# Strassen's seven block products for the Gelu half of two up-projections, with weight sums made by adding transfers

## The chip, the cores and the metric

One core of a Trainium2 chip runs the whole program. The metric is the device time in microseconds of one execution; several executions are made, and their median is given. The profile is of one execution, and its times are microseconds from the first instruction (ns where marked). TensorE (PE; PEld is its weight load) multiplies into PSUM banks, ScalarE (ACT) and VectorE (DVE) do the element work, GpSimd (POOL) and SyncE (SP) mostly issue transfers here.

## The reference, cut to what matters

A decoder trunk of two layers for 512 tokens of 1024 features: layer 0 mixes tokens by dilated attention, layer 1 by a gated recurrence, and each is followed by this block, wrapped in RMS norms and added to the residual stream:

```
def conv_ffn(x, w_up, conv_w, conv_b, w_down):
    u = causal_dwconv(x @ w_up, conv_w, conv_b)
    g, v = u[..., :D_FF], u[..., D_FF:]
    return (jax.nn.gelu(g, approximate=True) * v) @ w_down
```

`D_FF` is 3072, so `w_up` is 1024 x 6144. Its first 3072 columns feed the Gelu half, the others the value half. The convolution runs along the tokens and has three taps per feature.

## The kernel before

**Products in three passes.** An fp32 operand is split into a high part (`hi`, a ScalarE copy to fp32r) and the remainder (`lo`, a VectorE subtraction); `split` (L148) does both. A product is then hi x hi + hi x lo + lo x hi, three matmuls (`mm3`, L257). The activations `hT` are kept transposed, features on the partitions in 8 blocks of 128, the 512 tokens along the free side, and are split once per projection. The weights are split as they arrive.

**The weight stream.** `plan` lists all weight chunks in order. A chunk of the up-projection is 1024 x 256 (1 MB, one transfer by `load`, L193, on SP's queue, into one of three `raw` buffers). `pump` (L167) cuts a loaded chunk into two units of 1024 x 128, splits them (two instructions of 512 elements on ScalarE and two on VectorE per unit) and keeps up to eight units (`W_UNITS`). `take` hands out a unit, `done` gives its place back, and `tick` (L222), called after every output tile, steps the side jobs in `sides` and then calls `pump`. The schedule is manual: every engine works through its instructions in the order in which the program writes them, and waits are on what the program wrote before.

**The up-projection.** `ffn` (L591) runs over 12 pairs j: a Gelu chunk of 256 columns and the value chunk that belongs to it. `feat_tiles` (L433) makes four output tiles of 128 features x 512 tokens, each 8 x 3 matmuls into a PSUM bank of its own, of eight. In the first pair the tokens are halved, 256 columns a matmul. After each tile comes `sink` (L607): `conv` (L594) reads the bank with one ScalarE instruction and two VectorE ones; a Gelu tile then gets its activation on ScalarE (L611), a value tile is multiplied into the Gelu tile on VectorE (L615). The results `gv` (24 tiles) are split again for the down-projection, `rows_run` (L475), which takes 12 chunks of rows and ends in the norms that read and write the residual `x_sb`.

Small tiles of 512 columns come from a pool of 32 (`gen`); `gain` tiles hold norm weights; GpSimd's queue carries gains and the token transposes through memory.

Of the kernel before, what the change touches and what calls it, by code (L numbers as in the profile page):

```python
# [18 lines left out]
P = 128  # L19
S = 512  # L20
D = 1024
# [53 lines left out]
def kernel(  # L75
# [38 lines left out]
    def nm(s):  # L114
        uid[0] += 1
        return f"{s}{uid[0]}"
# [11 lines left out]

    ident = cp.tile([P, P], F32, tag="ident", name="ident")
    make_identity(nc, ident)  # L130
    x_sb = cp.tile([P, 4, D], F32, tag="x_sb", name="x_sb")

    def gain(src, layer, eng=nc.gpsimd):
        g = cp.tile([P, D], F32, tag="gain", name=nm("gain"), bufs=2)
# [19 lines left out]
    raws, units, pieces = {}, {}, []  # L154
    sides, first_w, first_y, one = [], [], [], []

    def parts_of(kind, raw):

        if kind == "feat":
            return [raw[:, :, m * P : (m + 1) * P] for m in range(2)]  # L160
        if kind == "value":
            return [raw[:, 2 * i : 2 * i + 2, :] for i in range(2)]
        if kind == "rows":
            return [raw[:, i : i + 1, :] for i in range(2)]
        return [raw]

    def pump(limit=2):  # L167

        for _ in range(limit):
            i = state["cv"]  # L170
            if not pieces and i < state["dma"]:
                pieces.extend((i, j, u) for j, u in enumerate(parts_of(plan[i][0], raws.pop(i))))
                state["cv"] += 1
            if pieces and state["live"] < W_UNITS:
                i, j, raw = pieces.pop(0)
                hi, lo = (
                    wp.tile([P] + list(raw.shape[1:]), F32R, tag=t, name=nm("w" + t)) for t in ("hi", "lo")
                )
                h = raw.shape[1] // 2
                cuts = [(slice(None), slice(0, h)), (slice(None), slice(h, 2 * h))]  # L180
                if raw.shape[1] == 1:
                    cuts = [(slice(None), slice(0, 1), slice(n, n + 512)) for n in (0, 512)]
                if plan[i][4] is not None:
                    split_normed(hi, lo, raw, plan[i][4] + (2 * j if plan[i][0] == "value" else 0))
                    cuts = []
                for c in cuts:
                    split(hi[c], lo[c], raw[c])
                units[i, j] = (hi, lo)
                state["live"] += 1
            while not pieces and state["dma"] < len(plan) and state["dma"] - state["cv"] < RAW_BUFS:  # L190
                load()

    def load():  # L193
        i = state["dma"]
        kind, kd, cols, srcs = plan[i][:4]
        raw = wp.tile([P, kd, cols], F32, tag="raw", name=nm("raw"), bufs=RAW_BUFS)
        at = 0
        for src, n in srcs:
            nc.sync.dma_start(raw[:, :, at : at + n] if kind == "value" else raw[:, at : at + n, :], src)
            at += n  # L200
        raws[i] = raw
        state["dma"] += 1

    def chunk():
        i = state["next"]
# [10 lines left out]
    def done(n=1):  # L216
        state["live"] -= n
# [16 lines left out]
        while sides:  # L234
            tick()

    def w_cols(w, c0, normed=False):
# [4 lines left out]
        plan.append(("feat", KD, 256, srcs, 0 if normed else None))  # L242

    def w_value(w, *cuts):

# [37 lines left out]
    def halves(ap):  # L283
        return [ap[:, 0:512], ap[:, 512:1024]]
# [28 lines left out]
        return t.rearrange("p (b n i) -> p n b i", b=4, i=32)  # L313

    def prenorm(t, hT, g, wait):
        xh, gh = halves(x_sb[:, t, :]), halves(g)
# [31 lines left out]
    def first_transposed(t, i):  # L348

        ps = psum("tr")  # L350
        for k in range(4 * i, 4 * i + 4):
            nc.tensor.transpose(
                ps[:, k % 4 * P : (k % 4 + 1) * P],
                x_sb[:, t, i * 512 : i * 512 + 512].rearrange("t (p k) -> t k p", k=4)[:, k % 4], ident,
            )
        first_split(t, i, ps)

# [14 lines left out]
    def first_squares(i):  # L372
        for t in range(4):
            junk = gen(s="junk")
            nc.scalar.activation(
                junk, x_sb[:, t, i * 512 : i * 512 + 512], AF.Square, accum_out=first_ss[i][:, t : t + 1]
            )

    def first_roots():
# [20 lines left out]
    def postnorm(t, banks, g, final):  # L400
        at = [slice(0, 512), slice(512, 1024)]
        parts = banks
        u = [gen(s="post") for _ in at]

        def gained(i):
            nc.vector.tensor_tensor(u[i], parts[i], g[:, at[i]], op=ALU.mult)

        y = rms(parts, gained)
        for i, c in enumerate(at):
            xc = x_sb[:, t, c]  # L410
# [180 lines left out]
    def ffn(layer, hT, post, pre):  # L591
# [25 lines left out]
        order = [([0, 1, 2, 3], range(9)), ([0], range(9, 12)), ([1], range(9, 12))]  # L617
        order += [([2, 3], [9]), ([2], [10, 11]), ([3], [10, 11])]
        prep, run = rows_proj(12, act_split(gv), order, post, pre)
        for j in range(12):  # L620
            if j == 11:
                prep(3)
            feat_tiles(2, hT, lambda b, ps: sink(b, ps, j), j == 0)
        return run()


    def attention(hT, post, pre):
# [436 lines left out]
    for layer in range(2):  # L1064
# [7 lines left out]
            for c in range(4):  # L1072
                w_rows(lru_w_out[0], c * 256)
        for j in range(12):
            w_cols(ffn_w_up[layer], j * 256)
# [12 lines left out]

    def x_half(t, i):
        c = slice(i * 512, (i + 1) * 512)  # L1090
        nc.sync.dma_start(x_sb[:, t, c], x[0, t * P : (t + 1) * P, c])

    def w_part(i, k0, k1):
        nc.sync.dma_start(raws[i][:, k0:k1, :], plan[i][3][0][0][:, k0:k1, :])
# [69 lines left out]
```

## Time and profile before

| | |
|---|---|
| median of 3 runs | 1455.94 us (1455.89 to 1456.03) |
| profiled execution | span 1454.0 us from first to last instruction; 1.9 us of the median lies around it |
| TensorE busy | 1445.0 us, 99% |
| VectorE / ScalarE / GpSimd busy | 61% / 46% / 9% |
| mean granted TensorE clock | 0.999 |
| read from / written to memory | 156.24 MB / 15.29 MB |

How to read the rows that follow: a group's row gives line, engine, operation, output<-inputs, shapes and count, then busy time and mean ns of one, then the idle time of its engine just before, with what ended it. A chain row gives start, length, and what. A window row gives, for a stretch, its length and each engine's busy time with its count, then the granted clock, the transfer engines' share and GB/s. A timeline row gives start, length, engine, line, operation and count, in brackets the idle time before and its releaser. A tile's row gives the shortest, median and longest duration in ns. A busy PE includes matmuls that overlap; what a matmul costs is read from the distance between starts.

### The profile page before, as it was taken

The numbers are of one execution on the slowest core, as the hardware profiler recorded it, in microseconds if no ns is written. First come the engines' busy times: TensorE is split into PE (matmuls) and PEld (weight loads), VectorE is DVE, ScalarE is ACT, GpSimd is POOL, SyncE is SP. The second block draws the span as 40 slices with busy tenths as digits, with TensorE's granted clock in tenths as the row PEclk, the third lists the DMA queues.
The fourth block names the chain that finished last, engine by engine and source line by source line (L and its number), as shares of the span: only waits on it lengthen the run. The fifth ranks groups of instructions, "written<-read, shape, count | busy, mean of one in ns | idle before, by whom it ended". The sixth has DMA issues, their size and how long they took to land.

```text
span 1454.0 us, 18793 instructions
## 1 busy us (share of the span) xinstructions
PE 1445.0 (99%) x6861; PEld 1214.4 (84%) x6861; DVE 879.8 (61%) x1955; ACT 675.9 (46%) x1532; POOL 133.9 (9%) x275
## 2 busy tenths in 40 slices
PE   9999999999999999999999999999999999999998
PEld 7888888888888898888888888888898888888886
DVE  6767747474735975555564338769775555564333
ACT  7656636262615553343444335589453434444221
POOL 0340414040402100000000001000100000000000
PEclk9999999999999999999999999999999999999999
DMA  7653637372726343323323322432333233223201
GB/s 225 207 146 109 174 113 208 104 215 97 216 96 211 102 131 100 103 87 102 101 88 116 115 73 88 131 116 84 120 102 116 87 102 102 87 104 128 88 0 58
DMA packets 125364, 172.76 MB, mean 119 GB/s; under 512 B 8736, under 2 KB 102392, under 8 KB 125272
## 3 DMA queue, kind: packets, MB, share of 16 engines
q1 hardware_dynamic: 114280, 145.48, 31.0%
q0 software_dynamic: 10144, 25.04, 5.9%
q8 instruction: 54, 0.88, 0.2%
q10 hardware_dynamic: 848, 1.05, 0.2%
q14 instruction: 38, 0.31, 0.1%
HBM read 156.24 MB, written 15.29 MB: 118 GB/s over the span
## 4 chain that ended last, share of the span: by engine, by line
PE 93%; ACT 4%; DVE 3%; issue 1%; DVEq 0%; ACTq 0%
PE ps L259 55%; PE acc L259 24%; PE v L758 8%; PE v L688 1%; DVE xb L967 1%; PE O L909 1%; PE S L854 1%; PE S L808 1%; DVE wlo L150 1%; ACT sig L988 1%; ACT whi L149 1%; PE O L259 1%; PE tr L341 1%; ACT sig L1007 0%; ACT a L1005 0%
## 5 line engine op out<-in xcount | busy, mean ns | idle before, releaser
L259 PE MATMUL ps<-hT,whi 128*128 128x512 f32 (+1 forms) x2752 | 801.3, 375 | 0.0
L259 PEld LDWEIGHTS ps<-hT,whi 128*128 128x128 f32 x2752 | 503.6, 188 | 91.6
L259 PE MATMUL ps<-hT,wlo 128*128 128x512 f32 (+1 forms) x1376 | 515.3, 374 | 0.0
L150 DVE TENSOR_TENSOR wlo<-raw,whi 128x512 fp32r<-128x512 f32 x360 | 230.8, 686 | 187.2 <-ACT whi L149 187.1
L259 PEld LDWEIGHTS ps<-hT,wlo 128*128 128x128 f32 x1376 | 259.1, 188 | 46.5
L149 ACT ACTIVATE whi<-raw 128x512 fp32r<-128x512 f32 x360 | 204.6, 621 | 135.4 <-PE acc L259 121.0
L600 DVE SCALAR_TENSOR_TENSOR u<-ps,cols,u 128x511 f32<-128x511 f32 x192 | 143.8, 749 | 140.6 <-ACT u L596 137.2
L259 PE MATMUL acc<-whi,ahi 128*128 128x512 f32 x512 | 199.7, 390 | 0.0
L259 PE MATMUL acc<-whi,alo 128*128 128x512 f32 x512 | 199.4, 389 | 0.1
L259 PE MATMUL acc<-wlo,ahi 128*128 128x512 f32 x512 | 199.3, 389 | 0.0
L143 ACT ACTIVATE whi<-raw,first_w 128x128 fp32r<-128x128 f32 (+1 forms) x432 | 146.2, 425 | 56.6 <-PE ps L259 33.9
L596 ACT ACTIVATE u<-ps,cols 128x512 f32<-128x512 f32 x96 | 74.8, 779 | 210.0 <-PE ps L259 210.0
L144 DVE SCALAR_TENSOR_TENSOR wlo<-raw,first_w,whi 128x128 fp32r<-128x128 f32 (+1 forms) x432 | 139.5, 389 | 1.4 <-ACT whi L143 1.3
L259 PEld LDWEIGHTS acc<-whi,alo 128*128 128x128 f32 x512 | 96.1, 188 | 20.5 <-DVE alo L150 0.5
L259 PEld LDWEIGHTS acc<-whi,ahi 128*128 128x128 f32 x512 | 96.1, 188 | 19.8
L259 PEld LDWEIGHTS acc<-wlo,ahi 128*128 128x128 f32 x512 | 96.2, 188 | 19.8
L758 PE MATMUL v<-whi,hT 128*128 128x512 f32 x320 | 102.4, 393 | 0.0
L302 POOL DMA_DIRECT2D turned<-T x36 | 19.6, 547 | 763.4 <-DVE T L296 759.9
L309 POOL DMA_DIRECT2D ft<-turned x144 | 78.7, 554 | 39.6 <-issue 17.7
L758 PEld LDWEIGHTS v<-whi,hT 128*128 128x128 f32 x320 | 60.1, 188 | 12.3
L611 ACT ACTIVATE u<-u 128x512 f32<-128x512 f32 x48 | 30.3, 632 | 80.4 <-DVE u L600 80.4
L758 PE MATMUL v<-wlo,hT 128*128 128x512 f32 x160 | 62.3, 389 | 0.0
(171 smaller groups left out, 1010.7 us busy)
## 6 DMA issues: line engine op xcount, KB each, us to landing
raw<-in_ffn_w_up_dram SPq DMA_DIRECT2D x48, 1024.0 KB
raw<-in_attn_w_qkv_dram SPq DMA_DIRECT2D x67, 512.0 KB
raw<-in_ffn_w_down_dram SPq DMA_DIRECT2D x24, 1024.0 KB
raw<-in_lru_w_in_dram SPq DMA_DIRECT2D x8, 1024.0 KB
turned<-T POOLq DMA_DIRECT2D x28, 256.0 KB, 2.6
ft<-turned POOLq DMA_DIRECT2D x112, 64.0 KB, 5.8
vrows<-v SPq DMA_DIRECT2D x16, 256.0 KB
vp<-vrows SPq DMA_DIRECT2D x16, 256.0 KB
```

Of the source, the lines that this page charges most:

```text
L143: nc.scalar.activation(hi[:, k], raw[:, k], AF.Copy, scale=w)
L144: nc.vector.scalar_tensor_tensor(lo[:, k], raw[:, k], w, hi[:, k].bitcast(F32), op0=ALU.mult, op1=ALU.subtract)
L149: nc.scalar.activation(hi, raw, AF.Copy)
L150: nc.vector.tensor_tensor(lo, raw, hi.bitcast(F32), op=ALU.subtract)
L259: mm(dst, l[a], r[b], start=start and n == 0, stop=stop and n == 2)
L302: nc.gpsimd.dma_start(d, T)
L309: nc.gpsimd.dma_start(t[32 * c : 32 * c + 32].rearrange("j (b x) -> j b x", b=4), d.rearrange("(b j) (c x) -> c j b x", j=32, c=4)[c],)
L341: nc.tensor.transpose(ps[:, k * P : (k + 1) * P], xs[i][:, k * P : (k + 1) * P], ident)
L596: nc.scalar.activation(u, ps, AF.Identity, scale=cc[:, j : j + 1], bias=cc[:, 48 + j : 49 + j])
L600: nc.vector.scalar_tensor_tensor(u[:, d:], ps[:, : S - d], wc, u[:, d:], op0=ALU.mult, op1=ALU.add)
L611: nc.scalar.activation(u, u, AF.Gelu_apprx_tanh)
L758: mm(banks[t], hT[a][:, k, t * P : (t + 1) * P], W[b][:, k % 2, :], start=(k, a, b) == (0, 0, 0), stop=(k, a, b) == (KD - 1, 1, 0),)
```

## The change

In pairs 3 to 10 of both up-projections the Gelu product (1024 x 256 weights by 1024 x 512 activations) is made from 2 x 2 blocks by seven block products, not eight, in Winograd's form. A block of the weights is 512 x 128, a block of the activations 512 x 256 tokens. Four sums of activation blocks (`T`) are made once per layer by a side job, `token_sums`, in place of the residual, which goes out to memory meanwhile and comes back before pair 11 (`x_back`). Four sums of weight blocks are made per pair: `c += d` by an adding transfer from memory when the chunk is loaded, `a += c` and `b += a` by adding transfers within SBUF, and `a - d` by VectorE. The Gelu chunk then has four units, made in the order first value unit, `first`, `second`, `third`, `fourth`, second value unit. The products share two PSUM banks, `y[0]` and `y[1]`: the left 256 columns accumulate, are copied, negated and go on accumulating (`p5`, `z`, `c()` from `-a()`), and the right 256 columns are written by VectorE. Between the products stand the value chunk's quarters a to h (six matmuls of 512 columns each).

```diff
+SEVEN = range(3, 11)
...
+    def summed(i, raw):
+
+        a, b, c, d = (raw[:, 4 * k : 4 * k + 4, m * P : m * P + P] for m, k in ((0, 0), (0, 1), (1, 0), (1, 1)))
+        shape = [KD, P]
+
+        def first(hi, lo):
+            two = [h.rearrange("p (k m) c -> p k (m c)", m=2) for h in (hi, lo)]
+            split(*two, raw[:, 0:4, :])
+            add_rows(a, c)
+
+        def second(hi, lo):
+            split(hi, lo, raw[:, :, 0:P])
+            add_rows(b, a)
+            nc.vector.tensor_tensor(a, a, d, op=ALU.subtract)
+
+        def third(hi, lo):
+            split(hi, lo, raw[:, :, 0:P])
+
+        def fourth(hi, lo):
+            split(hi[:, 0:4], lo[:, 0:4], d)
...
         for _ in range(limit):
             i = state["cv"]
-            if not pieces and i < state["dma"]:
-                pieces.extend((i, j, u) for j, u in enumerate(parts_of(plan[i][0], raws.pop(i))))
-                state["cv"] += 1
+            if not pieces and i + (i < len(plan) and plan[i][0] == "wino") < state["dma"]:
+                if plan[i][0] == "wino":
+                    u, v = summed(i, raws.pop(i)), [
+                        plain(i + 1, j, r) for j, r in enumerate(parts_of("feat", raws.pop(i + 1)))
+                    ]
+                    pieces.extend([v[0], *u, v[1]])
+                    state["cv"] += 2
...
+        if kind == "wino":
+            add_rows(raw[:, 0:4, P:256], srcs[0][0][:, 4:8, P:256])
         raws[i] = raw
         state["dma"] += 1
+
+    def add_rows(to, src):
+        nc.gpsimd.dma_start(to, src, accum_op=ALU.add)
...
         for j in range(12):
+            if j == 1:
+                side(token_sums(hT, T))
             if j == 11:
+                x_back()
                 prep(3)
-            feat_tiles(2, hT, lambda b, ps: sink(b, ps, j), j == 0)
+            if j in SEVEN:
+                seven(hT, T, lambda b, ps: sink(b, ps, j))
+            else:
+                feat_tiles(2, hT, lambda b, ps: sink(b, ps, j), j == 0)
         return run()
 
+    kept = []
+
+    def x_back():
+
+        X[0] = cp.tile([P, 4, D], F32, tag="x_sb", name=nm("x_sb"))
+        nc.gpsimd.dma_start(X[0], kept.pop())
+
+    def token_sums(hT, T):
+
+        assert len(sides) == 1
+        d = dp.tile([P, 4, D], F32, name=nm("x_kept"))
+        nc.gpsimd.dma_start(d, X[0])
+        kept.append(d)
+        homes = cp.tile([P, 4, D], F32R, tag="x_sb", name=nm("T"))
+        homes = [homes[:, n] for n in range(4)]
+        homes += [cp.tile([P, D], F32R, tag="gain", name=nm("T"), bufs=2) for _ in range(2)]
+        homes = [[h[:, 0:512], h[:, 512:1024]] for h in homes]
+        homes += [[gen(F32R, "T") for _ in range(2)] for _ in range(2)]
+        homes = [[h.rearrange("p (k t) -> p k t", k=2) for h in hs] for hs in homes]
+        yield 1
+
+        def both(k0, n):
+            o = gen(s="B").rearrange("p (k t) -> p k t", k=2)
+            hi, lo = (h[:, k0 : k0 + 2, n * 256 : n * 256 + 256] for h in hT)
+            nc.gpsimd.tensor_tensor(o, hi.bitcast(F32), lo.bitcast(F32), op=ALU.add)
+            return o
+
+        tt = nc.vector.tensor_tensor
+        B = {}
+        for k in range(2):
+            for n, at in (((0, 0), 2 * k), ((0, 1), 2 * k), ((1, 1), 4 + 2 * k), ((1, 0), 4 + 2 * k)):
+                B[k, n] = both(at, n[1])
+        yield 2
+        for k in range(2):
+            b11, b12, b22, b21 = (B[k, n] for n in ((0, 0), (0, 1), (1, 1), (1, 0)))
+            tt(b11, b11, b12, op=ALU.subtract)
+            tt(b12, b12, b22, op=ALU.subtract)
+            tt(b22, b22, b11, op=ALU.add)
+            tt(b21, b21, b22, op=ALU.subtract)
+            yield 1
+            for n, b in enumerate((b11, b22, b12, b21)):
+                split(homes[2 * n][k], homes[2 * n + 1][k], b)
+            if not k:
+                yield 1
+        T.extend([homes[2 * n], homes[2 * n + 1]] for n in range(4))
+
+    def seven(hT, T, sink):
+
+        i, iv = chunk(), chunk()
+        t = gen(s="part")
+        y, v = {}, {}
...
+        left = {
+            1: (0, pairs(0), block(0, 0), 0), 5: (0, pairs(1), turn(0), 1), 6: (1, row(0), turn(1), 1),
+            2: (1, row(4), block(1, 0), 0), 7: (2, row(0), turn(2), 1), 3: (2, row(4), block(1, 1), 1),
+            4: (3, row(0), turn(3), 1),
+        }
+
+        def product(n):
+            u, l, r, b = left[n]
+            W = take(i, u)
+            if b not in y:
+                y[b] = psum()
+            for k in range(4):
+                for q, (wa, ha) in enumerate(PASSES):
+                    mm(
+                        y[b][:, 0:256], l(W[wa], k), r(ha, k), start=n in (1, 5) and k == q == 0,
+                        stop=k == 3 and q == 2, skip_group_check=True,
+                    )
...
+        a, c = (lambda: y[0][:, 0:256]), (lambda: y[1][:, 0:256])
+        p5, z = t[:, 0:256], t[:, 256:512]
+        for step in "5a13bc62d7ef4gh":
+            if step in "1234567":
+                n = int(step)
+                product(n)
+                if n == 5:
+                    nc.scalar.activation(p5, c(), AF.Copy)
+                elif n == 1:
+                    done()
+                elif n == 3:
+                    nc.scalar.activation(z, c(), AF.Copy)
+                    nc.scalar.activation(c(), a(), AF.Copy, scale=-1.0)
+                elif n == 6:
+                    nc.vector.tensor_tensor(y[0][:, 256:512], z, c(), op=ALU.subtract)
+                elif n == 2:
+                    done()
+                    sink(0, y[0])
+                elif n == 7:
+                    done()
+                    nc.vector.tensor_tensor(y[1][:, 256:512], c(), p5, op=ALU.subtract)
+                else:
+                    done()
+                    sink(1, y[1])
+            else:
+                n = "abcdefgh".index(step)
+                quarter(n)
+                if n % 4 == 3:
+                    done()
+                    sink(2 + n // 4, v[n // 4])
+            tick()
```

More of the change, by code (lines that the diff above doesn't have):

```diff
@@ L155, with plain, f @@
     sides, first_w, first_y, one = [], [], [], []
+    def plain(i, j, raw):
+        def f(hi, lo):
+            h = raw.shape[1] // 2
+            cuts = [(slice(None), slice(0, h)), (slice(None), slice(h, 2 * h))]
+            if raw.shape[1] == 1:
+                cuts = [(slice(None), slice(0, 1), slice(n, n + 512)) for n in (0, 512)]
+            if plan[i][4] is not None:
+                split_normed(hi, lo, raw, plan[i][4] + (2 * j if plan[i][0] == "value" else 0))
+                cuts = []
+            for c in cuts:
+                split(hi[c], lo[c], raw[c])
+        return (i, j), list(raw.shape[1:]), f
+    def summed(i, raw):
[13 more added lines that the diff above has]
+            split(hi[:, 0:4], lo[:, 0:4], d)
+        return [((i, n), shape, f) for n, f in enumerate((first, second, third, fourth))]
     def parts_of(kind, raw):
@@ L170, in pump @@
             i = state["cv"]
[L171 to L188 removed]
+            if not pieces and i + (i < len(plan) and plan[i][0] == "wino") < state["dma"]:
[6 more added lines that the diff above has]
+                else:
+                    pieces.extend(plain(i, j, r) for j, r in enumerate(parts_of(plan[i][0], raws.pop(i))))
+                    state["cv"] += 1
+            if pieces and state["live"] < W_UNITS:
+                key, shape, fill = pieces.pop(0)
+                hi, lo = (wp.tile([P] + shape, F32R, tag=t, name=nm("w" + t)) for t in ("hi", "lo"))
+                fill(hi, lo)
+                units[key] = (hi, lo)
                 state["live"] += 1
@@ L1074 @@
         for j in range(12):
-            w_cols(ffn_w_up[layer], j * 256)
+            w_cols(ffn_w_up[layer], j * 256, kind="wino" if j in SEVEN else "feat")
             w_cols(ffn_w_up[layer], D_FF + j * 256)
```

33 lines of the change are left out of this document (25 added, 8 removed).

## The prediction

> **What bounds the kernel now.** I read the page first, then the chain of waits, then the two up-projections alone, then the single instructions in them.
>
> ```profile
> span 1454.0 us, 18793 instructions
> PE 1445.0 (99%) x6861; PEld 1214.4 (84%) x6861; DVE 879.8 (61%) x1955; ACT 675.9 (46%) x1532; POOL 133.9 (9%) x275
> PE 93%; ACT 4%; DVE 3%; issue 1%; DVEq 0%; ACTq 0%
> 500.13 5.75 PE ps L259 x48
> 510.50 253.77 PE ps L259 x1176
> 1062.99 253.77 PE ps L259 x1176
> core 0: us, PE busy (x) PEld busy (x) DVE busy (x) ACT busy (x) POOL busy (x), PEclk, DMA share, GB/s
> 532.00:553.76 21.76, 21.76 (x97) 18.02 (x96) 14.21 (x23) 8.44 (x14) 0.00 (x0) 1.00 0.41 135
> ```
>
> The end is set by TensorE. Both up-projections are one piece each of the chain, 253.77 us without a wait. The window is one chunk pair (a Gelu chunk and its value chunk): 96 matmuls of 512 columns in 21.76 us, 226.7 ns each, with VectorE busy 14.2 us and ScalarE 8.4 us in it. The 48 matmuls in 5.75 us have 256 columns (the halved first pair): 119.8 ns each. Half the columns cost 53%, not 50%.
>
> **What is removed from TensorE.** Per pair, 48 matmuls of 512 columns (10.88 us) become 7 products x 4 x 3 = 84 of 256 columns (10.06 us). The value chunk keeps its 48. The pair needs 20.94 us of TensorE, 0.82 us less; 16 pairs give 13.1 us. That is all there is to win, 0.9%.
>
> **What is added, and where.** The instructions' durations:
>
> ```profile
> L596 ACT ACTIVATE u<-ps,cols 128x512 f32<-128x512 f32 x96 | 74.8, 779 | 210.0 <-PE ps L259 210.0
> L600 DVE SCALAR_TENSOR_TENSOR u<-ps,cols,u 128x511 f32<-128x511 f32 x96 | 71.9, 749 | 137.2 <-ACT u L596 137.2
> L611 ACT ACTIVATE u<-u 128x512 f32<-128x512 f32 x48 | 30.3, 632 | 80.4 <-DVE u L600 80.4
> L615 DVE TENSOR_TENSOR u<-u,u 128x512 f32<-128x512 f32 x48 | 33.2, 692 | 1.6
> L149 ACT ACTIVATE whi<-raw 128x512 fp32r<-128x512 f32 x360 | 204.6, 621 | 135.4 <-PE acc L259 121.0 <-PE ps L259 14.4
> L150 DVE TENSOR_TENSOR wlo<-raw,whi 128x512 fp32r<-128x512 f32 x360 | 230.8, 686 | 187.2 <-ACT whi L149 187.1
> L830 ACT ACTIVATE phi<-ft x16: 402/518/633, 75.3 to 191.3; 128x512 fp32r<-128x512 f32 x8, 128x256 fp32r<-128x256 f32 x8
> L831 DVE TENSOR_TENSOR plo<-ft,phi x16: 416/553/693, 79.3 to 192.1; 128x512 fp32r<-128x512 f32 x8, 128x256 fp32r<-128x256 f32 x8
> 570.85 0.69 DVE L615 TENSOR_TENSOR u<-u,u 128x512 f32<-128x512 f32 x1
> 571.46 1.29 DVE L150 TENSOR_TENSOR wlo<-raw,whi 128x512 fp32r<-128x512 f32 x2
> 573.91 0.78 ACT L596 ACTIVATE u<-ps,cols 128x512 f32<-128x512 f32 x1 [3.62 <-PE ps L259]
> 574.72 1.54 DVE L600 SCALAR_TENSOR_TENSOR u<-ps,cols,u 128x511 f32<-128x511 f32 x2 [1.98 <-ACT u L596]
> 576.35 0.63 ACT L611 ACTIVATE u<-u 128x512 f32<-128x512 f32 x1 [1.66 <-DVE u L600]
> ```
>
> L830 and L831 give both sizes: 256 elements take 0.40 and 0.42 us, 512 take 0.63 and 0.69, so 1024 (no row has it) about 1.08 on ScalarE and 1.24 on VectorE by the same slope. A seven-product pair adds to ScalarE 3 x 1.08 + 0.62 in place of 4 x 0.62 for the weight splits, and three 256-column copies (p5, z, -a; 1.2 us): +2.6 us, about 11 in all. VectorE gets 3 x 1.24 + 0.69 for 4 x 0.69, the subtraction a-d (0.69) and two 256-column subtractions (0.84): +3.7 us, about 18. Neither sum exceeds 20.94. By busy time the change fits; the order of the queues is another matter.
>
> Each engine takes its work in the order it is written. The last rows show it: Gelu (L611) stands behind its conv on VectorE, and ScalarE idles 1.66 us for it though splits are waiting. The order follows from the ticks. Eight weight units are held, a tick refills what was given back, and a seven-product pair uses six units. Following the step string "5a13bc62d7ef4gh" with that rule: "first" is made after h, "second" after product 1, "third" after product 2, "fourth" after d, the second value unit after 7, the next pair's first value unit after 4. Two things in it put foreign work ahead of TensorE:
>
> (1) "second" splits on ScalarE what a+=c writes, and that add waits for both splits of "first". Behind it on ScalarE are z and -a, for which product 6 waits.
>
> (2) In "second", a-d overwrites what b+=a reads, so VectorE stands still for that transfer. Behind it is z-c, and product 2, which writes the other half of z-c's bank. c-p5 likewise stands ahead of product 4, behind two evacuations.
>
> Whether a wait goes by bank or by address, this stretch of before shows:
>
> ```profile
> 213.48 1.95 PE L854 MATMUL S<-qk,qk 128*128 128x128 f32 x16
> 214.57 0.29 DVE L796 CUSTOM_DVE_ANT_0 L<-S,toe 128x128 f32<-128x128 f32 x1 [3.54 <-PE S L854]
> ```
>
> Two banks of four 128-column blocks are written; VectorE, idle 3.54 us, reads the first block only. It starts 1.09 us after the first matmul, when half of the 1.95 us (the first bank's four blocks) is over, not after 0.25. So this program's waits go by bank, and I count product 2 behind z-c. With waits by address product 2 would not stand behind z-c, and a pair would be about 2.4 us shorter (rival C).
>
> **The transfers.** No accumulating transfer and none within SBUF is in the trace. The nearest are on the same queue:
>
> ```profile
> turned<-T POOLq DMA_DIRECT2D x28, 256.0 KB, 2.6
> ft<-turned POOLq DMA_DIRECT2D x112, 64.0 KB, 5.8
> DMA to landing us min/median/max: 2.0/5.1/8.8
> ```
>
> Each add moves 256 KB in 512 pieces of 512 bytes and must read its target too. Below: 2.0 us, the shortest landing. Above: 5.8 us, the median of the 512-byte gathers, which queue behind each other. I take L = 3.5 us: the 2.6 us of the plain 256 KB transfer plus about a microsecond for the second read and the shorter pieces. A gain from an add is excluded, since the trace has no add that it replaces.
>
> The Trainium skill (DMA: Bandwidth & Descriptors, section "Anatomy of one DMA") puts a GpSimd-issued transfer at about 2.0 us plus its bytes at 436 GB/s, an estimate of 2.6 us for 256 KB whatever is done with them; the plain row agrees. By that rule the sum below would come to 16 x 7.4 = 119 us, 1575.
>
> **One pair, followed round.** Without L:
> - product 4, its landing (0.39 us of a matmul, in the row at 1446.93 below, less the pitch of 0.23), conv, Gelu of tile 1: 1.44 + 0.2 + 0.78 + 1.5 + 0.63 = 4.55
> - ScalarE two splits of the value unit (1.04) and conv (0.78); VectorE the rest of conv 1.5, multiply 0.69, low half of "first" 1.24: 5.25
> - a+=c: L. Then "second", 1.08 + 1.24: 2.3
> - b+=a: L. Then a-d and z-c: 1.1
> - product 2 and landing 1.64; conv 0.78 + 1.5, Gelu 0.63, "third" 1.08 + 1.24: 6.9
> - VectorE: conv of value tile 2 1.5, multiply 0.69, "fourth" 0.69, c-p5 0.42: 3.3; then product 4 again.
>
> That is 23.4 us and some twenty hand-overs of about 0.05 us (574.72 after 573.91 + 0.78 is 0.03): 24.4. Neighbours on one engine overlap by about 0.1 us at four places (571.46 after 570.85 is 0.61, not 0.69), so 24.0 + 2 L. With L = 3.5 a pair takes 31.0 us, not 21.76: +9.2 us. TensorE then idles 31.0 - 20.9 = 10.1 us a pair in three places, before products 6, 2 and 4, about 3 us each.
>
> The first of the eight pairs is dearer (its sums start late, behind the token sums), the last cheaper (no sums left to make); I count all alike. 16 x 9.2 = 148 us.
>
> **Costed at nothing.** The 1 MB loads have the share 0.41 of the transfer engines in the quoted window, and SP's queue has nothing else in it. The add c+=d is issued at load time and used a pair later; GpSimd, empty in the window, waits in it for the load, with a+=c behind, which the loads' lead covers; without that cover some of a pair's two loads (0.41 x 21.76 = 9 us) would be added to L. Token sums put eight splits and sixteen VectorE operations, about 5 and 11 us, into pairs 1 and 2, where VectorE has 2 x 7.5 us free; eight GpSimd adds have no row: at three times VectorE's 0.69 they take 17 us, and the two ticks of 5.44 us before their readers cover all but 6 us, which that same slack takes, once per layer. x goes out and back, 2 MB each, 15 us at the window's 135 GB/s; it is next needed after nine chunks of the down-projection (9 x 4 tiles x 12 matmuls at 226.7 ns = 98 us), and the gains behind it on GpSimd's queue then too. Without that cover it is those 15 us per layer.
>
> **Sum.** 1454.0 + 148 = 1602 for the span. The median of the runs is 1455.94, 1.9 above it: 1604 us.
>
> **Rivals.**
>
> A, faster: everything added is hidden and TensorE keeps its 13.1 us: 1443 us. For it: busy times fit, and units are made eight ahead, so a late split alone costs nothing. Against: the round is 24.0 us even with L = 0, over 20.94; it would need z, -a, z-c and c-p5 not to stand behind the fills. 0.04.
>
> B, slower still: the clock falls in the new gaps.
>
> ```profile
> 1446.93 0.39 PE L259 MATMUL acc<-whi,alo 128*128 128x512 f32 x1
> 1446.00:1450.00 4.00, 1.32 (x6) 0.75 (x4) 2.72 (x9) 1.67 (x5) 0.00 (x0) 1.00 0.24 90
> 1450.00:1454.00 4.00, 0.00 (x0) 0.00 (x0) 0.81 (x2) 0.00 (x0) 0.00 (x0) 0.82 0.35 131
> ```
>
> After the last matmul (ends 1447.3) the clock stays full past 1450; a mean of 0.82 over the last 4 us, at half clock, puts the fall at about 1452.6, 5.2 us of idleness. The gaps here are 3 to 4 us, so probably not; if L is 5 or more, they reach it. Products 2 and 4 would each take 1.44 us longer: 46 us more, 1650; with L = 5 alone 1652. The Trainium skill (TensorE: Matmul & The Clock Gate, section "Why this matters for your kernels") gives gaps over about 3 us as enough; the 5.2 us here doesn't contradict it if the fall waits for a whole window. 0.17 for 1635 and more.
>
> C, slower by less: waits by address, or quick adds. By address 16 x 2.4 us less, 1565; L = 2.0 gives 16 x 6.24 = 100, 1556. 0.18 for under 1575.
>
> D, no change, gain and waits cancelling: the round would have to be 21.76 us. 0.01.
>
> **Numbers.** The forecast, L between 2.6 and about 4.5, has 0.60; B 0.17, C 0.18, A 0.04, D 0.01. The range 1548 to 1668 takes in L = 2.0 (1556) and L = 5 (1652) and leaves out A and the far ends of B and C. Faster by over 0.2% (about what a measurement here can tell from no change) 0.04, same 0.01, slower 0.95.
>
> **What would show it.** Right: the up-projections lengthen from 254 to some 330 us each and the rest stays; TensorE's idle time is released by ScalarE's -a and VectorE's z-c and c-p5; VectorE waits longest for the b+=a transfer, ScalarE for a+=c. Wrong in size: landings of the adds far from 3.5 us. Wrong in kind: a pair under 21.76 us, or idle time in front of product 2 that ends with a weight unit.

## The result, and the profile after

The changed kernel takes 1685.72 us (median of four runs, 1684.17 to 1688.12) against 1455.91 us for the kernel before: ratio 1.158, 95% interval 1.1564 to 1.1597. It is slower by 229.8 us. I had forecast 148 us more, and the range ended at 1668.

The page of the changed kernel, the same parts as shown of before, and TensorE's granted clock in forty slices:

```profile
span 1682.6 us, 20368 instructions
PE 1503.2 (89%) x7437; PEld 1279.1 (76%) x7437; DVE 964.4 (57%) x2035; ACT 717.5 (43%) x1596; POOL 217.8 (13%) x343
PEclk9999999999999888789999999999978787889999
PE 59%; DVE 14%; DMA 14%; ACT 7%; issue 5%; POOL 1%; DVEq 0%; POOLq 0%; ACTq 0%
```

The chain that ended last was TensorE's for 93% of the span; now it is for 59%. VectorE, transfers and ScalarE share most of the rest. The clock dips in two places, which are the two up-projections. Which waits these are, the chain of waits and the view of waits say:

```profile
ACT whi L150 <- DMA raw<-raw: 135.7, 16, 14.5
DVE raw L186 <- DMA raw<-raw: 74.9, 16, 5.0
PE ps L751 <- ACT ps L776: 58.0, 14, 6.5
PE ps L751 <- DVE ps L778: 48.4, 16, 3.7
PE ps L751 <- DVE ps L784: 38.0, 16, 3.2
PE ps L751 <- ACT T L150: 19.1, 4, 5.5
```

Columns: who waited for whom, us in total, times, longest. The first two rows are "second" waiting for a+=c on ScalarE (L150 splits) and a-d waiting for b+=a on VectorE (L186). The next three are TensorE before product 6 (behind -a, L776), product 2 (behind z-c, L778) and product 4 (behind c-p5, L784). These are the three places and the three releasers that the prediction names. The fourth, products waiting for T, it had put at nothing.

The transfers, from the view of DMA issues (median us to landing last) and from one steady pair's timeline (start, us, instruction, the idle time before it):

```profile
raw<-raw POOLq DMA_DIRECT2D x32, 256.0 KB, 4.2
raw<-in_ffn_w_up_dram POOLq DMA_DIRECT2D x16, 256.0 KB, 4.6
627.46 1.22 DVE L151 TENSOR_TENSOR wlo<-raw,whi 128x1024 fp32r<-128x1024 f32 x1
629.06 1.27 POOL L243 DMA_DIRECT2D raw<-raw  x1 [0.68 <-DVE wlo L151]
633.29 1.06 ACT L150 ACTIVATE whi<-raw 128x1024 fp32r<-128x1024 f32 x1 [6.84 <-DMA raw<-raw]
```

From the end of the low half of "first" (628.68) to the start of "second" (633.29) there are 4.6 us: 0.38 before the issue, 4.15 to the landing, 0.08 to the reader. I had put 3.5 us there.

The two stretches of seven-product pairs by windows. For each layer: pair 3 (from the end of pair 2), pairs 4 to 9, pair 10. Columns as in the prediction's window; the seventh is the granted clock.

```profile
568.44:622.76 54.32, 28.94 (x133) 24.52 (x133) 31.39 (x45) 19.45 (x33) 3.85 (x3) 0.72 0.31 74
622.76:829.87 207.11, 150.69 (x793) 131.64 (x792) 91.48 (x126) 64.02 (x103) 21.76 (x17) 0.84 0.38 83
829.87:855.14 25.27, 21.48 (x133) 18.94 (x132) 15.36 (x24) 11.53 (x22) 1.64 (x3) 1.00 0.75 260
1233.60:1287.80 54.20, 29.02 (x134) 24.65 (x133) 31.39 (x45) 19.45 (x33) 3.87 (x3) 0.75 0.32 75
1287.80:1496.62 208.82, 152.74 (x794) 133.57 (x792) 91.49 (x126) 63.75 (x103) 21.90 (x17) 0.82 0.37 82
1496.62:1523.50 26.88, 23.09 (x134) 20.34 (x133) 15.37 (x24) 12.32 (x23) 1.12 (x2) 0.94 0.71 250
```

Sixteen pairs take 576.6 us where sixteen at 21.76 take 348.2. The difference, 228.4, is the whole change of the span (228.6). A steady pair is 34.7 us (415.9 / 12), the first of a layer 54.3, the last 26. Against 31.0 us for each, the miss lies here: 2 x 23.3 = 46.5 us in pairs 3, 12 x 3.66 = 43.9 us in the steady ones, and 9.9 us less in pairs 10.

### The profile page after: what moved, and what is told of

The parts are those of the page before. It is cut to its first block, busy times and chain, and to the rows that moved or that the text cites. A ratio compares the mean times of both kernels' runs of the same rounds, so it can differ in the third digit from the quotient of the medians.

```text
span 1682.6 us, 20368 instructions
## 1 busy us (share of the span) xinstructions
PE 1503.2 (89%) x7437; PEld 1279.1 (76%) x7437; DVE 964.4 (57%) x2035; ACT 717.5 (43%) x1596; POOL 217.8 (13%) x343
## 4 chain that ended last, share of the span: by engine, by line
PE 59%; DVE 14%; DMA 14%; ACT 7%; issue 5%; POOL 1%; DVEq 0%; POOLq 0%; ACTq 0%
PE ps L300 22%; PE acc L300 21%; DMA raw<-raw 8%; PE v L928 6%; DVE wlo L151 6%; DMA raw<-in_ffn_w_up_dram 5%; DVE u L641 5%; PE ps L751 4%; ACT whi L150 2%; PE v L858 1%; DVE xb L1137 1%; ACT u L637 1%; ACT u L652 1%; PE O L1079 1%; PE S L1024 1%
## 5 line engine op out<-in xcount | busy, mean ns | idle before, releaser
L300 PE MATMUL ps<-hT,whi 128*128 128x512 f32 (+1 forms) x2240 | 656.2, 378 | 0.0
L300 PEld LDWEIGHTS ps<-hT,whi 128*128 128x128 f32 x2240 | 410.2, 193 | 68.1
L151 DVE TENSOR_TENSOR wlo<-raw,whi 128x512 fp32r<-128x512 f32 (+1 forms) x360 | 269.7, 787 | 290.1 <-ACT whi L150 290.0
L300 PE MATMUL ps<-hT,wlo 128*128 128x512 f32 (+1 forms) x1120 | 420.2, 375 | 0.0
L150 ACT ACTIVATE whi<-raw 128x512 fp32r<-128x512 f32 (+1 forms) x360 | 226.9, 679 | 287.5 <-DMA raw<-raw 135.7
L300 PEld LDWEIGHTS ps<-hT,wlo 128*128 128x128 f32 x1120 | 214.1, 191 | 38.6
L751 PE MATMUL ps<-T,whi 128*128 128x256 f32 x512 | 120.3, 332 | 122.3 <-ACT ps L776 58.0
L751 PEld LDWEIGHTS ps<-T,whi 128*128 128x128 f32 x512 | 98.9, 231 | 140.4 <-ACT ps L776 63.9
L751 PE MATMUL ps<-hT,whi 128*128 128x256 f32 x384 | 88.1, 330 | 48.4 <-DVE ps L778 48.4
L751 PEld LDWEIGHTS ps<-hT,whi 128*128 128x128 f32 x384 | 74.1, 233 | 54.4 <-DVE ps L778 52.9
```

The source lines that it names most:

```text
L150: nc.scalar.activation(hi, raw, AF.Copy)
L151: nc.vector.tensor_tensor(lo, raw, hi.bitcast(F32), op=ALU.subtract)
L300: mm(dst, l[a], r[b], start=start and n == 0, stop=stop and n == 2)
L751: mm(y[b][:, 0:256], l(W[wa], k), r(ha, k), start=n in (1, 5) and k == q == 0, stop=k == 3 and q == 2, skip_group_check=True,)
```

## The experiments

My theory after the result: a steady pair is the in-order round of the prediction, 24.0 us plus two transfers, but a transfer holds its reader 4.6 to 5 us, and the gaps lower the clock; pair 3 is dear by way of GpSimd, whose queue and whose additions I had costed at nothing. Rivals: products slower than matmuls, engines simply full, token sums dear by themselves, the clock as the main term. All runs below stand beside runs of the kernel before at 1455.8 us.

**Token sums alone (e1).** The weights' kind goes back to "feat", and every chunk runs as before; token_sums and x_back stay.

```diff
-            if j in SEVEN:
-                seven(hT, T, lambda b, ps: sink(b, ps, j))
-            else:
-                feat_tiles(2, hT, lambda b, ps: sink(b, ps, j), j == 0)
+            feat_tiles(2, hT, lambda b, ps: sink(b, ps, j), j == 0)
```

> Keeps the token sums, the trip of x out to memory and back and the splits of T, but all 12 Gelu chunks run as before; T is not used. Theory 1 (the extra time is made by the weight sums' transfers, each waited for in order; the token sums are dear only because the adds queue behind them on GpSimd and VectorE): here nothing queues behind GpSimd, and eight units are made ahead, so the time stays near the kernel before, 1456 to 1468 us. Rival (the token sums cost by themselves the 25 us by which pair 3 of each layer is longer than the forecast): about 1506 us.

1457.07 us, ratio 1.0009 (0.9999 to 1.0018). As expected by the theory: the additions, the splits of T and x's way out and back cost 1.3 us at most when nothing waits behind them. The timeline still shows a collision:

```profile
513.46 10.26 POOL L695 TENSOR_TENSOR B<-hT,hT 128x512 f32<-128x512 f32 x6
513.98 8.58 DVE L151 TENSOR_TENSOR wlo<-raw,whi 128x512 fp32r<-128x512 f32 x5
```

Five VectorE splits that take 0.65 us each elsewhere take 8.58 us beside GpSimd's additions. TensorE doesn't notice, since the units are made eight ahead.

**Token additions on VectorE (e2)**, in the changed kernel:

```diff
-            nc.gpsimd.tensor_tensor(o, hi.bitcast(F32), lo.bitcast(F32), op=ALU.add)
+            nc.vector.tensor_tensor(o, hi.bitcast(F32), lo.bitcast(F32), op=ALU.add)
```

> The changed kernel with one word altered: the eight token additions of each layer run on VectorE instead of GpSimd. Theory 1: pair 3 is dear (56 us against 34.5) because GpSimd works on the additions for 10.5 us, one of VectorE's multiplies stands 9.2 us beside them, and the first a+=c is issued only behind them. Then pair 3 falls to about 38 to 45 us, the whole by 20 to 36 us, to 1650 to 1666 us. Rival (pair 3 is late because of the 2 MB spill beside the loads, and c+=d waits for its load ahead of a+=c on the queue): within 8 us of 1686.

1669.06 us, ratio 1.146 (1.1443 to 1.1477): 16.7 us less. This is between the two expectations (20 less, or 8 and fewer): the additions on GpSimd are a part of pair 3's excess, not most of it.

**No weight sums (e3).** All four removed, c+=d and a-d among them; everything else stays on the unsummed weights.

> The changed kernel without any weight sum: no c+=d, a+=c, b+=a, and no a-d; the splits, the seven products, the copies and the token sums all stay, on unsummed weights. Theory 1 (in-order round of 24.0 us plus two transfers plus half clock): the waits for transfers and the idle time that lowers the clock go, and what is left is the order of the fills on ScalarE and VectorE. By the same steps without transfers a pair takes about 25 us (range 23 to 26.5), the whole 1456 + 16 x 3.2 = about 1507 us (1485 to 1530). Rival (the products themselves are slower than the plain matmuls, or the two engines are simply too busy): over 1560 us. Rival (all was the transfers): 1443 us.

1531.09 us, ratio 1.0514 (1.0497 to 1.0532), one microsecond over the expected range. A steady pair takes 26.1 us instead of 34.7, pair 3 only 28. So the sums and their transfers cause two thirds of the loss, 155 of 230 us. What is left, 75 us, comes with the order and the clock: TensorE still waits 2.9 us in each pair for c-p5. What I hadn't expected is that 2.9 us are enough to lower the clock, in eight of the twelve steady pairs:

```profile
612.00:614.90 2.90, 2.90 (x14) 2.08 (x12) 1.43 (x2) 2.90 (x5) 0.00 (x0) 1.00 0.00 0
614.90:617.80 2.90, 0.01 (x1) 0.00 (x0) 2.83 (x6) 0.76 (x2) 0.00 (x0) 1.00 0.00 0
617.80:618.50 0.70, 0.63 (x5) 0.64 (x6) 0.70 (x3) 0.00 (x0) 0.00 (x0) 1.00 0.00 0
618.50:621.50 3.00, 3.00 (x13) 2.71 (x13) 0.86 (x2) 0.78 (x1) 0.00 (x0) 0.50 0.96 307
```

TensorE works, is idle for 2.9 us, works again, and only 0.7 us later goes to half clock for 3 us. Pairs without the fall take 25.03 us, pairs with it 26.6.

**Two additions on VectorE (e4).** a+=c and b+=a as VectorE instructions, at the same places:

```diff
-            add_rows(a, c)
+            nc.vector.tensor_tensor(a, a, c, op=ALU.add)
...
-            add_rows(b, a)
+            nc.vector.tensor_tensor(b, b, a, op=ALU.add)
```

> The changed kernel with a+=c and b+=a as two VectorE additions of 512 elements a partition (about 0.69 us each) in the place where the transfers were issued; c+=d stays a transfer. Theory 1: each transfer of 4.15 us and more that was waited for becomes 0.69 us, the clock stays up, a pair takes 25 to 26 us, the whole about 1515 us (1500 to 1540). Rival (VectorE, busy about 19.5 of 21 us, becomes the bound, or c+=d holds the queue): over 1560 us. Rival (the transfers were hidden by units made ahead): above 1650 us.

1556.61 us, ratio 1.0688 (1.0673 to 1.0704), over the expected range. Its steady pairs are as expected (26.0 us, no more than the 26.1 without any sum), so VectorE has room for both additions. The excess is in pair 3, 41 us from its first product on, and the timeline shows why:

```profile
546.47 1.29 POOL L243 DMA_DIRECT2D raw<-in_ffn_w_up_dram  x1 [15.71 <-DVE u L641]
547.18 11.65 DVE L151 TENSOR_TENSOR wlo<-raw,whi 128x1024 fp32r<-128x1024 f32 x1
547.27 10.47 POOL L698 TENSOR_TENSOR B<-hT,hT 128x512 f32<-128x512 f32 x8
559.59 1.06 ACT L150 ACTIVATE whi<-raw 128x1024 fp32r<-128x1024 f32 x1 [11.53 <-DVE raw L181]
```

GpSimd's queue stands 15.71 us before it can issue c+=d. Only then do the eight additions run, at 547 instead of 513 us as in the first experiment. They meet the splits of the weight sums, and one VectorE split of 1.22 us takes 11.65. ScalarE idles 11.53 us for the addition behind it.

**Both together (e11)**, e4 and e2:

> The changed kernel with a+=c, b+=a and the token additions on VectorE, in its own order of units and steps (e4 and e2 together). Theory 1: in e4 the eight token additions on GpSimd ran late (547 to 558 us, behind a c+=d that waited for its load) and one VectorE operation stood beside them for 11.65 us instead of 1.22, which made pair 3 take 41 us. Without that, pair 3 takes about 28 us as without any weight sum, and the whole comes to the time of e3, 1531 us (1522 to 1540); what is left to e8_reordered, 83 us, is the order alone. Rival (the additions themselves delay pair 3): 1550 us or more.

1538.12 us, ratio 1.0566 (1.055 to 1.0582). As expected: 18.5 us less than e4, pair 3 at 31 to 32 us, steady pairs 26.1.

**The subtraction later (e5).** The transfers stay, but a-d stands at the start of "third", behind z-c and product 2:

```diff
         def second(hi, lo):
...
-            nc.vector.tensor_tensor(a, a, d, op=ALU.subtract)
...
         def third(hi, lo):
+            nc.vector.tensor_tensor(a, a, d, op=ALU.subtract)
             split(hi, lo, raw[:, :, 0:P])
```

> The changed kernel with a-d moved from 'second' to the start of 'third', so that VectorE no longer stands still for the transfer b+=a with z-c behind it. Theory 1: the 3.7 us of idle time before product 2 goes, and with it the half clock in that product; 'third' still has to wait for b+=a, so part of it comes back before product 7. A pair falls from 34.5 to 30.5 to 32 us, the whole to about 1640 us (1620 to 1655). Rival (the wait only moves to 'third'): within 8 us of 1686.

1641.14 us, ratio 1.1268 (1.1249 to 1.1286), as expected: 44.6 us for one line moved. The wait before product 2 falls from 48.4 us in all to this:

```profile
PE ps L751 <- DVE ps L778: 9.5, 16, 0.6
```

**One addition on VectorE (e7)**, b+=a alone:

> The changed kernel with b+=a alone as a VectorE addition, a+=c and c+=d as transfers. Theory 1 (each waited transfer costs its 4.15 us in every pair): a pair takes 34.5 - (4.15 - 0.69) - 1.5 of half clock in product 2 = 29.5 us (28.5 to 31), the whole about 1612 us (1590 to 1635), a little over half of the way from 1686 to the 1557 of the kernel with both additions on VectorE. Rival (the two transfers overlap, so that one of them is enough to hold the pair): over 1650 us.

1641.34 us, ratio 1.1276 (1.1259 to 1.1293). It misses its range by 6 us. A steady pair takes 31.9 us, not 29.5. One transfer is gone, but the remaining gap before product 6 is followed by ten microseconds at half clock:

```profile
625.50:628.80 3.30, 0.00 (x0) 0.00 (x0) 0.00 (x0) 0.93 (x1) 0.00 (x0) 0.98 0.72 88
628.80:638.80 10.00, 8.55 (x32) 7.68 (x33) 4.54 (x6) 1.77 (x5) 0.00 (x0) 0.50 0.01 2
```

Products 6 and 2 follow each other with only 0.6 us between them here, so both are late by it: 6.25 us from the start of 6 to the end of 2, against 3.7 in a pair at full clock of e3. These 2.55 us are about what the pair takes more than I expected (31.9 - 29.5 = 2.4). I had expected the half clock to go with the transfer; it stayed.

**Gaps filled (e6, then e9).** Extra matmuls keep TensorE busy before products 6 and 2, and in a second run before product 4 too:

```diff
                 n = int(step)
+                if n in (6, 2):
+                    if 1 not in v:
+                        v[1] = psum()
+                    for _ in range(12):
+                        mm(v[1], hT[0][:, 0, 0:P], hT[0][:, 0, :], start=True, stop=True)
                 product(n)
```

> The changed kernel with 12 extra 128x512 matmuls (2.7 us at 226.7 ns) into the second value bank before product 6 and 12 more before product 2 of each pair; their result is overwritten by the value chunk's first matmul. They fill the gaps of 3.9 and 3.7 us. Theory 1 with the clock as a part of it: products 6 and 2 (2.5 to 2.9 us at half clock in the changed kernel) take 1.5 us again, and the pair gets about 1.5 us shorter: about 1662 us (1648 to 1674), although TensorE has 43 us more work in all. Rival (the clock costs nothing, since products 6 and 2 are not what ends late): 1686 or, where the extra matmuls are in the way, more.

> As e6_fill_gaps, with 10 further extra matmuls (2.3 us) before product 4 of each pair, into the bank that product 2's evacuation has set free. In e6 the clock stayed up in products 6 and 2 (1.7 us each) and fell in the gap before product 4 instead (product 4 took 2.93 us). Theory 1: with all three gaps filled the clock stays at 1.00, product 4 and the two quarters behind it take 1.6 and 2.9 us, and a pair is 1.3 to 2.5 us shorter than in e6: 1655 to 1680 us. What is left above the kernel before is then waiting alone. Rival (products are not late by the clock, the extra matmuls only add work): 1695 us or more.

1694.92 us, ratio 1.1644 (1.1624 to 1.1664), and 1683.45, ratio 1.1564 (1.1546 to 1.1581): both above what I expected, the first as its rival had it. A pair with all three gaps filled, to be held against 622.76:829.87 above (0.84):

```profile
622.91:656.33 33.42, 29.48 (x168) 25.11 (x167) 15.25 (x21) 10.74 (x18) 3.82 (x3) 1.00 0.40 87
```

In this pair the clock is back at 1.00, and the twelve steady pairs average 34.05 us instead of 34.66. So filling gains 0.6 us of a steady pair, net of what the extra matmuls cost. Product 6 may run at half speed, since z-c waits on VectorE for b+=a anyway; in four of the twelve pairs product 2 still falls. In the run with two gaps the fall moved on to the third (product 4 takes 2.93 us). And in pair 10, which has no gap before products 6 and 2, 24 extra matmuls are 5.4 us of plain work, 11 us in both layers, which I had forgotten in both expectations. How much the extra matmuls delay the products in the other pairs these two runs can't separate.

**Order (e8).** The additions and token additions on VectorE; "first" made ahead of the value unit; value quarters where ScalarE and VectorE work on product 3 and 6; Gelu issued after the tick's fill:

```diff
-                    pieces.extend([v[0], *u, v[1]])
+                    pieces.extend([u[0], v[0], u[1], u[2], u[3], v[1]])
...
-                nc.scalar.activation(u, u, AF.Gelu_apprx_tanh)
+                if j not in SEVEN:
+                    nc.scalar.activation(u, u, AF.Gelu_apprx_tanh)
+                else:
+                    gelus.append(u)
...
-        for step in "5a13bc62d7ef4gh":
+        for step in "5a1bc3ef6g724dh":
...
             tick()
+            for u in gelus:
+                nc.scalar.activation(u, u, AF.Gelu_apprx_tanh)
+            gelus.clear()
```

> Attempt to keep the seven products' gain: a+=c, b+=a and the token additions on VectorE; 'first' is made ahead of the first value unit; the steps in the order 5a1bc3ef6g724dh, with value quarters between product 3 and 6 and products 2 and 4 late; the Gelu of a seven-product chunk is issued after the fill of its tick. Theory 1: with no transfer in the round and the quarters placed where z, -a, z-c and c-p5 are being made, TensorE has no gap, a pair takes 20.94 us, and the whole is 1443 to 1450 us. Rival (VectorE, busy about 19.5 us of a pair's 20.9, is the bound of such a pair): 1456 to 1480 us.

1447.72 us, ratio 0.9945 (0.9932 to 0.9957): faster than the kernel before. Every steady pair takes 20.96 us.

**The same order with the transfers back (e10):**

> e8_reordered with a+=c and b+=a as transfers again; the order of units and steps, the later Gelu and the token additions on VectorE stay. Theory 1: 'first' is now made earlier and product 6 and 7 come later, so that part of each transfer is covered, but 'second' still waits for a+=c and a-d for b+=a: a pair takes 26 to 29 us, the whole about 1545 us (1520 to 1580). Rival (the order alone was the cause; once it is right, transfers are covered): 1443 to 1455 us. Rival (order does nothing for the transfers): over 1620 us.

1575.51 us, ratio 1.0833 (1.0815 to 1.0851), in the expected range; a pair takes 29.5 us. Starting from the 1669 of e2, which has the same token additions, the order alone brings 94 us, the two additions on VectorE alone 131 us (e11), both together 221 us. Neither suffices by itself.

**Two quarters first (e12).** The step string of e8 as "ab51c3ef6g724dh":

> e8_reordered with the steps in the order ab51c3ef6g724dh: two value quarters ahead of product 5. In e8 the steady pairs take 20.96 us, but the first product of pair 3 waits some 2 to 4 us per layer for T. Theory 1: the two quarters (2.7 us) cover that wait, the steady pairs stay at 20.96, and the time is 1442 to 1446 us. Rival (the wait moves on to the next products or the steady pairs lose their cover): 1447 us or more.

1444.29 us, ratio 0.9921 (0.9906 to 0.9936), as expected. This is the best version, 0.8% faster than the kernel before. Its page's chain, and one of its pairs by windows:

```profile
PE 92%; ACT 4%; DVE 3%; issue 1%; DVEq 0%; ACTq 0%
613.13:634.07 20.94, 20.94 (x134) 18.98 (x132) 16.68 (x23) 10.82 (x18) 1.28 (x1) 1.00 0.42 114
```

TensorE is busy for the whole of a 20.94 us pair. The 11.5 us gained are what rival A counted (13.1) less 1.6 us. The token sums alone cost 1.3 us in the first experiment, which may be most of it; that is not tested.

## Why the prediction was right or wrong

**TensorE's own gain: right.** 20.94 us a pair was worked out, and 20.94 us is what the last version's pairs take. So rival A was no mistake of arithmetic; what it asked for, z, -a, z-c and c-p5 not standing behind the fills, took another order and neither a+=c nor b+=a as a transfer.

**Busy times: right in what they say, too high in number.** VectorE is busy 15.24 us of a steady pair (91.48 / 6), not about 18; ScalarE 10.67, about the 11 predicted. The prediction's terms for VectorE add up to 3.2 us more, not the 3.7 written there. And the window of before that I started from held 14.21 us of VectorE work; the mean of its eight pairs is 98.98 / 8 = 12.37, and 12.37 + 3.2 is close to what was measured:

```profile
568.43:742.51 174.08, 174.08 (x770) 144.20 (x769) 98.98 (x144) 68.41 (x112) 0.00 (x0) 1.00 0.30 97
```

**The round in order: right.** The three gaps and their releasers came out as named: 3.8, 3.4 and 2.2 us per steady pair before products 6, 2 and 4, where I had put about 3 each. The waits for T are the gap I hadn't put anywhere. The up-projections became 368 us (253.8 and half of 228.4), not 330. The sign that VectorE waits longest for b+=a and ScalarE for a+=c isn't met to the letter. These are their longest waits for a transfer (27.7 and 43.2 us in the steady pairs of layer 0), but both engines wait longer for another engine that stands behind the same transfers:

```profile
ACT u L637 <- PE ps L751: 79.6, 12, 9.3
DVE wlo L151 <- ACT whi L150: 54.8, 18, 6.7
```

The 24.0 us fit: a steady pair less its two transfers and less what product 2 loses by the clock (both below) is 34.66 - 9.65 - 1.17 = 23.8 us. That pairs of e4 at full clock take 25.03 us, near 24.0 and two additions of 0.69, doesn't show it. Pairs of e3, without any addition, take the same 25.03, and in both the chain runs through TensorE from product 5 to 6, not through "first" and "second". The wait by bank stands as read: product 2 waited behind z-c, which writes the other half of its bank. Rival C, waits by address or quick adds, falls with that and with the landings.

**The transfer, L = 3.5 us: too small, the first failed step.** In the twelve steady pairs a+=c holds its reader 4.96 us on average (4.58 to 5.58) and b+=a 4.69 (4.59 to 5.02), counted from the end of the low half before it to the start of the reader. The sum is 9.65 us instead of 7.0: 2.65 us a pair, 32 of the 82 us missed. I had taken the landing of the plain transfer (2.6) and added a microsecond. The landing is 4.15 even alone, and I had left out the 0.45 us before the issue and before the reader. The estimate of 2.6 us from the Trainium skill (DMA: Bandwidth & Descriptors, section "Anatomy of one DMA") holds for the plain row and is 1.5 us short for these adds. a+=c is slower than b+=a where it is issued right behind c+=d on GpSimd's queue, which I had costed at nothing.

The loads' lead, which the prediction trusted, is gone in the steady pairs too. A load starts only when VectorE has split the last unit of the buffer that it fills, late in the pair before. In eight of the twelve steady pairs the chain that ended last passes through the load, mostly by c+=d to a+=c; start, length, what:

```profile
688.42 7.82 DMA raw<-in_ffn_w_up_dram
696.95 0.82 POOL raw L243
697.77 5.14 DMA raw<-raw
```

Here this costs little: a+=c is issued 0.36 to 0.63 us after the low half of "first" in these pairs (0.36 us is usual), and its slower landing is in the 4.96 us above.

**"I count all alike": the second failed step.** I wrote that the first pair is dearer and dropped it from the sum. It takes 54.3 us, 23.3 over the forecast; twice per kernel 46.5 us. The way through it, one row of the changed kernel's chain and then its timeline:

```profile
530.10 12.39 DMA raw<-in_ffn_w_up_dram
546.65 1.29 POOL L243 DMA_DIRECT2D raw<-in_ffn_w_up_dram  x1 [16.11 <-DVE u L656]
547.45 10.49 POOL L698 TENSOR_TENSOR B<-hT,hT 128x512 f32<-128x512 f32 x8
549.28 9.21 DVE L656 TENSOR_TENSOR u<-u,u 128x512 f32<-128x512 f32 x1
557.62 1.60 POOL L243 DMA_DIRECT2D raw<-raw  x1
562.16 1.06 ACT L150 ACTIVATE whi<-raw 128x1024 fp32r<-128x1024 f32 x1 [14.48 <-DMA raw<-raw]
592.97 1.28 POOL L243 DMA_DIRECT2D raw<-in_ffn_w_up_dram  x1 [26.90 <-DMA raw<-in_ffn_w_up_dram]
```

c+=d stands on GpSimd's queue for its load, the token additions behind it, a+=c behind them, "second" 14.48 us behind that on ScalarE, and the splits of T behind "second". That c+=d waits for its load is read, not printed, in the second row: the VectorE multiply named there ends in that moment, but c+=d needs nothing of it, while the load's bytes arrive until 546.0; the next c+=d (last row) names its load. The load ahead of it takes 12.39 us beside x's way out, where the one at 586.99 takes 5.31; I had trusted the loads' lead. Here "costed at nothing" failed in both parts: the queue, and the additions. Their duration I had overestimated (10.5 us measured, 17 guessed); that they stop VectorE I had not thought of. The Trainium skill states it (SBUF — State Buffer, section "Who interferes with whom": a VectorE instruction with two SBUF inputs contends with a GpSimd instruction that reads SBUF); the trace agrees, with 9.21 us for an instruction of 0.69. e2 and e11 show what the additions are worth, 17 to 18.5 us of the 46.5, and e1 that they cost 1.3 us at most when no weight sums follow. The rest of pair 3 goes when the sums' transfers go (54 to 28 us in e3, 31 to 32 in e11). How it divides between the wait for T, late loads and the queue I have read from the trace but not tested.

**The clock: rival B was right that it falls; the gap I asked for was too long, and the price was too high.** I read an idle time of 5.2 us as needed; gaps of 2.9 us (e3) suffice, and in e9 one of 1.85:

```profile
707.90:709.75 1.85, 0.02 (x2) 0.01 (x1) 1.03 (x2) 0.00 (x0) 0.00 (x0) 1.00 0.14 15
709.87:713.30 3.43, 3.43 (x15) 3.24 (x16) 0.00 (x0) 0.69 (x1) 0.00 (x0) 0.50 0.03 5
```

The end of the trace shows when the clock fell, not the shortest gap that makes it fall. The Trainium skill's figure of about 3 us (TensorE: Matmul & The Clock Gate, section "Why this matters for your kernels") was the better guide, though these gaps are shorter still. The free-running window of about 3.4 us that the Trainium skill gives (the same page, Part 1) agrees with spells of about 3.4 and 10 us and with a gap of one length that does it in one pair and not in the next.

What a spell costs depends on whether the slowed product is on the chain. Product 2 is, in the changed kernel (first row) and in e9 (second row):

```profile
641.29 2.94 PE ps L751 x12
641.86 1.71 PE ps L751 x12
```

In the twelve steady pairs product 2 takes 2.86 us on average, and 1.69 at full clock: 1.17 us a pair, 14 us in all. Product 4 falls in three of these pairs only, and product 6 costs nothing. B had put 1.44 us on each of products 2 and 4 in every pair, 46 us; its time of 1650 came out of a term three times too large. That product 2's loss passes on whole to the pair is read from the chain, not tested by itself. e9 gave 0.6 us a pair: product 2 still falls in four of its pairs (1.98 us on average, 0.88 less), and a+=c holds its reader 5.18 us instead of 4.96. In e3 a fall costs 1.6 us, on product 4 and the two quarters behind it, and in e7 about 2.5, on products 6 and 2.

**Together:** 32 (transfers) + 14 (clock) + 46.5 (pairs 3) - 9.9 (pairs 10, where less is waited for) = 83 us, where 82 were missed. That it closes to a microsecond is partly luck: the 24.0 us of the round are good to about 0.2 us a pair.

## What to carry to other kernels

A change that saves TensorE's work but sends each step through other engines' queues has to be followed round once in the order in which those queues take the work: busy times said it fits, and it does fit, but only after the order was changed. Price a transfer by what its reader loses, from the end of its writer to the start of its reader, and where the operation has no row of its own, take the upper end. A pair that differs from the others (the first, the last) is computed by itself, not noted and dropped. Half clock is priced only for the work that the chain passes through.

## What the runs showed of the hardware

An accumulating transfer of 256 KB takes 4.15 us from issue to landing where a plain one on the same queue took 2.6, and GpSimd is occupied 1.27 us to issue it. The plain one goes to memory in rows of 2 KB, the adding one stays within SBUF in pieces of 512 bytes; which of these differences makes the 1.5 us the runs don't separate. GpSimd's eight additions (1.3 us each) held one VectorE instruction for all of their 10.4 us, not for one of them (e4); in e1 five splits did get through beside six additions, and why is open. A gap of 2.9 us in TensorE's work, once of 1.85, can cost a spell of half clock that begins after the work has resumed; a gap of 4.3 us cost 10 us of it (e7).
